# A hybrid decoder layer on one core: merge projection in three column passes with kept weights, first FFN-out group of five f-tiles, four f-tiles in the last stage

## The chip, the cores and the metric

The kernel runs on 1 core of one Trainium2 chip (trn2). The metric is the device time of one execution in microseconds (us), lower is better; for the kernel before it is the median of three runs. The engines are TensorE (PE; PEld is its weight load), VectorE (DVE), ScalarE (ACT), GpSimd (POOL) and SyncE (SP, which issues the transfers here).

## The reference

One inference step of a one-layer decoder trunk: 1024 prompt columns and 8 samples, width 1024, FFN width 2816. All in float32. The mixers (a Conformer convolution and a gated delta rule) are not touched by the change; what follows them is:

```
merged = jax.nn.sigmoid(m_a) * y_a + jax.nn.sigmoid(m_b) * y_b
x = x + gt1 * (merged @ w_merge_out)
h2 = rms_norm(x, norm2_g) * (1 + sc2) + sh2
gate, up = jnp.split(h2 @ w_ffn_in, 2, axis=-1)
x = x + gt2 * ((jax.nn.silu(gate) * up) @ w_ffn_out)
...
y = rms_norm(x, final_norm_g)
```

## The kernel before

Activations lie transposed: channels on 128 partitions, T = 1032 columns (8 samples, then the prompt). Width 1024 is 8 tiles, the FFN has 22 f-tiles. A float32 product is done as three matmuls on rounded operands, high x high, high x low, low x high (`passes`); so each weight and each activation needs a `split`: ScalarE writes the high half (L188), VectorE subtracts for the low half (L189). Columns are worked in three passes of 344 (`cols(n)`). A `product` of eight k-tiles is 24 matmuls of 344 columns.

Weights come through the class `Weights`: there is one buffer `raw` for what SP loads, `prepare` splits it and only then is the next load asked for; the halves go into a ring of two (`whi`, `wlo`) or, for a kept weight ("hl"), into slots `whk`, `wlk`. `get` hands out the next one. SP, VectorE, ScalarE and GpSimd run what a scheduler has put in order; PE's order is that of the code; in the last stage the orders of VectorE, ScalarE and GpSimd are written by hand too. `along` holds generators of side work (norms, output); `after()` and `unit()` step them between products, and a `yield` says how many steps to wait.

The stages that matter, in the order of time:

- Merge projection (`merge`): for each output tile m a product with `w_merge_out`, `residual` into x2 (L1284, with L1287 and L1288 for the samples), a square and its sum for the norm (`Norm.square`, L1300 and L1304), and a write of x2 to a DRAM tile `xD`. Columns 0 and 1 are done for all m first, then column 2. Six weights have to be found again for column 2: two were kept split (`WMO_HL`), two are still in the ring, four were kept unsplit (`WMO_RAW`) and are split a second time ("again").
- norm2: `sums` (16 matmuls, L1315 and L1316), `rstd`, `bcast` (8 matmuls, L1326), then `modulate2` writes h2 = ms. Columns 0 and 1 together, then column 2.
- FFN in (`seven`, L1494): each f-tile of `silu(gate) * up` is written to a DRAM tile `aD`, since it doesn't stay on the chip.
- FFN out: f-tiles in groups `FGROUPS`; the tiles of a group are read back (`act_load`: a DMA into `ub`, `act` or `ar`, then a split into `ah` and `al`), then for each output tile and column pass one product over the group and a residual. While a group runs, the tiles of the next are read back. x2 is read back from `xD` (`x2_load`, in the order `XO`).
- Last stage: the last `FL` f-tiles (weights `wfl`), in three column blocks of 400, 400 and 232 (L1656), each with residual, square and sum; the final norm and the output multiply (`finish`, L1642) of a block run beside the next block; the last block is multiplied at the end from `yl` (L1680).

Of the kernel before, what the change touches and what calls it, by code (L numbers as in the profile page):

```python
# [18 lines left out]
P = 128  # L19
NP = 1024  # L20
NS = 8
T = NP + NS
# [10 lines left out]
FGROUPS = (7, 6, 6)  # L33
# [3 lines left out]
WMO_RAW, WMO_HL = (0, 1, 2, 3), (4, 5)  # L37
AHEAD = 3
XO = (0, 4, 1, 5, 2, 6, 3, 7)
WFL_AT = (1, 3, 5)  # L40
# [24 lines left out]
def trunk_step(ctx, tc, I, O):  # L65
# [136 lines left out]
    order += [(I["wmo"][m], 1024, "raw" if m in WMO_RAW else "hl" if m in WMO_HL else "") for m in range(KD)]  # L202
    order += [(None, 1024, "again") for m in WMO_RAW]
# [3 lines left out]
    for i, nf in enumerate(FGROUPS):  # L207
        for m in range(KD):
            order2.append((I["wfo"][m][:, f0 * P:(f0 + nf) * P], nf * P))
            if i == len(FGROUPS) - 1 and m in WFL_AT:  # L210
                order2.append((I["wfl"][WFL_AT.index(m)], 1024, "hl"))
        f0 += nf

    class Weights:


        def __init__(self, order):
            self.order, self.loaded, self.ready, self.kept, self.at = order, [], [], [], 0

        def load(self):  # L220
            if self.at < len(self.order) and not self.loaded:
                src, n, kind = (self.order[self.at] + ("",))[:3]
                self.at += 1
                if kind == "again":
                    raw = self.kept.pop(0)
                else:
                    raw = slot_d("rawk") if kind == "raw" else wp.tile(
                        [P, 1024], F32, tag="aw" if kind == "aw" else "raw", name="raw", bufs=1)
                    SP.dma_start(raw[:, :n], src)
                self.loaded.append((raw, n, kind))  # L230

        def prepare(self, eng=V):
            if self.loaded and not self.ready:
                raw, n, kind = self.loaded.pop()
                if kind == "hl":
                    hi, lo = slot_d("whk", F32R), slot_d("wlk", F32R)
                else:
                    hi = wp.tile([P, 1024], F32R, tag="hi", name="whi")
                    lo = wp.tile([P, 1024], F32R, tag="lo", name="wlo")
                split(hi[:, :n], lo[:, :n], raw[:, :n], eng)  # L240
                if kind == "raw":
                    self.kept.append(raw)
                self.ready.append((hi, lo))
                self.load()
# [28 lines left out]
    def after():  # L273
        W.prepare()
# [1070 lines left out]
    def modulate2(cs):  # L1345

        c0, c1 = cs[0].start, cs[-1].stop
        c = slice(max(c0, NS), c1)
        for k in range(KD):
            yield 0  # L1350
            sh = mods[:, SH2, k, :]
            modulate(x2[k], norm2.rb, a2[:, k, :], sh, ms[k][0], ms[k][1], x2[k], c0, c1, V)
            A.activation(x2[k][:, c], x2[k][:, c], AF.Identity, bias=sh[:, 0:1])
# [9 lines left out]
    kept = {}  # L1363
    for m in range(KD):
        w = W.get()
        if m not in WMO_RAW:
            kept[m] = w
        for n in range(2):
            merge(m, w, n)
            after()  # L1370
    add(norm2.work((cols(0), cols(1)), modulate2), 0)
    late = [6, 7, 0, 1, 2, 3, 4, 5]
    norm2.first, norm2.last = late[0], late[-1]
    for m in late:
        w = kept.pop(m) if m in kept else W.get()
        after()
        merge(m, w, 2)
# [169 lines left out]
    def act_load(f, sl, raw=None):  # L1547
        raw = slot_l("ar") if raw is None else raw
        hi, lo = sl("ah", F32R), sl("al", F32R)
        SP.dma_start(raw, aD[f])  # L1550
        split(hi, lo, raw, V)
        acts.append((hi, lo))

# [6 lines left out]
    for f in range(NPL, NF + 1):  # L1560
# [5 lines left out]
        if f > NPL:  # L1566
# [14 lines left out]
            if f == NF:  # L1581

                act_load(6, slot_d, act[NF - 2])
                x2_load(XO[1:6])
            seven(f - 1, "S4", B22, c12)
            SP.dma_start(aD[f - 1], a_)
            if f == NF - 1:
                for i in range(4):
                    act_load(i, slot_h, (v, a_)[i % 2])
            if f == NF:  # L1590
                x2_load(XO[6:])
        if f < NF:
# [14 lines left out]
            if f == NF - 1:  # L1607
                for i in range(4, 6):
                    act_load(i, slot_d, (ub[NF % 2], act[NF - 2])[i % 2])
# [11 lines left out]
    for g, nf in enumerate(FGROUPS):  # L1621
        for m in range(KD):
            w = W.get()
            for n in range(3):
# [5 lines left out]
            if m < ahead[g]:  # L1630
                sl = slot_h if (m < 4 if g + 1 < len(FGROUPS) else m < 2) else slot_d
                act_load(f1 + m, sl)
# [5 lines left out]
    def finish(cs):  # L1638
        c = cs[0]
        for k in range(KD):  # L1640
            yield 1 if c.start == 0 or k < 2 else 0.5
# [6 lines left out]
    norm3 = Norm(range(KD), V, slot_h)  # L1648
    yl = [slot_h(f"yl{i}")[:, :4 * YL].rearrange("p (k t) -> p k t", k=4) for i in range(2)]
    for a, b in ((0, YC), (YC, 2 * YC), (2 * YC, T)):  # L1650
# [12 lines left out]
        if b < T:  # L1663
            unit()
            add(norm3.work((c,), finish, 2, 2), 1)
# [9 lines left out]
    left(3)  # L1675
# [3 lines left out]
    for i in range(2):  # L1679
        V.tensor_tensor(yl[i], yl[i], ps[:, None, :YL].broadcast_to((P, 4, YL)), ALU.mult)  # L1680
        SP.dma_start(O["y"][:, 4 * i:4 * i + 4, c], yl[i])
# [93 lines left out]
```

## Time and profile before

| what | value |
|---|---|
| median of three runs | 1593.66 us (1591.69 to 1596.32) |
| the profiled execution's own time | 1594.41 us |
| its span, first to last instruction | 1592.7 us |
| mean granted clock of TensorE | 0.981 of full speed |
| merge projection to the FFN, about | 745 to 855 us |
| FFN-out groups | 1298.6 to 1538.0 us |
| last stage | 1538.0 to 1592.7 us |

Views of one profiled execution give start times from the span's beginning. A granted clock of 1.00 is 2.4 GHz, one of 0.50 is 1.2 GHz. An engine's idle time is given in square brackets before an instruction, with what ended it.

### The profile page before, as it was taken

Reading aid. Unit: us, or ns where it says so; the run is one execution under the profiler, and the core shown is the slowest. Engines: PE = TensorE matmul, PEld = TensorE weight load, DVE = VectorE, ACT = ScalarE, POOL = GpSimd, SP = SyncE. Lnnn points to the kernel's source line nnn. Section 1 sums busy time; section 2 is a strip of 40 time slices with the busy share of each in tenths; the row PEclk is TensorE's granted clock in tenths of the full one; section 3 lists DMA queues with packets and bytes.
Section 4 is the critical chain, followed back from the end, with each engine's and each line's share of the span. In section 5 each row is a group of like instructions: output and inputs, shape, how many; then the busy total and the mean of one; then the engine's idle time right before and its main releaser. Section 6 shows DMA issues by size and latency. Waiting matters only on the chain.

```text
span 1592.7 us, 27503 instructions
## 1 busy us (share of the span) xinstructions
PE 1525.4 (96%) x11383; PEld 1460.2 (92%) x11383; DVE 988.2 (62%) x1958; ACT 571.8 (36%) x1025; POOL 37.6 (2%) x67
## 2 busy tenths in 40 slices
PE   6999999999999999999979999999999978999996
PEld 3888999998888889999979999999999967999996
DVE  3667776999993642227466766666666754344446
ACT  5785653234334512114254433333333322021113
POOL 1210000000030000000000000000000000000000
PEclk8999999999999999999999999999999988999998
DMA  9134333233433444115202122222222164141202
GB/s 370 41 105 105 117 101 91 80 88 107 128 111 114 160 140 143 40 53 182 73 35 71 67 81 80 81 80 80 81 81 80 54 247 144 45 130 54 81 19 107
DMA packets 83374, 161.18 MB, mean 101 GB/s; under 512 B 20113, under 2 KB 41265, under 8 KB 83249
## 3 DMA queue, kind: packets, MB, share of 16 engines
q1 hardware_dynamic: 83248, 159.43, 30.8%
q8 instruction: 89, 1.46, 0.4%
q14 instruction: 37, 0.30, 0.1%
HBM read 128.37 MB, written 31.04 MB: 100 GB/s over the span
## 4 chain that ended last, share of the span: by engine, by line
PE 80%; DVE 10%; DMA 4%; ACT 4%; issue 1%; POOL 1%; SPq 0%; DVEq 0%; ACTq 0%; POOLq 0%
PE mm L264 49%; PE mm L1494 25%; DVE ca L719 3%; DVE cv L546 1%; PE ada L974 1%; DMA act<-aD 1%; PE w L791 1%; DVE wlo L189 1%; DMA x<-xD 1%; DVE x L1284 1%; DMA adw<-in_wada_dram 1%; DMA x<-in_x_dram 1%; ACT sq L1300 1%; DVE sacc L1304 0%; DMA em<-gcd 0%
## 5 line engine op out<-in xcount | busy, mean ns | idle before, releaser
L264 PE MATMUL mm<-hh,whi 128*128 128x344 f32 x920 | 306.1, 333 | 0.0
L264 PE MATMUL mm<-hl,whi 128*128 128x344 f32 x920 | 296.1, 322 | 0.0
L264 PE MATMUL mm<-hh,wlo 128*128 128x344 f32 x920 | 295.5, 321 | 0.0
L264 PEld LDWEIGHTS mm<-hh,whi 128*128 128x128 f32 x920 | 174.1, 189 | 14.8 <-issue 13.5
L1494 PE MATMUL mm<-mh,fm 128*128 128x258 f32 x960 | 182.7, 283 | 0.0
L264 PEld LDWEIGHTS mm<-hl,whi 128*128 128x128 f32 x920 | 174.2, 189 | 0.0
L264 PEld LDWEIGHTS mm<-hh,wlo 128*128 128x128 f32 x920 | 174.1, 189 | 0.0
L188 ACT ACTIVATE whi<-raw 128x1024 fp32r<-128x1024 f32 (+2 forms) x78 | 78.3, 1004 | 244.2 <-PE mm L264 219.3
L264 PE MATMUL mm<-ah,whi 128*128 128x344 f32 x456 | 148.0, 325 | 15.1 <-ACT ah L188 12.5
L189 DVE TENSOR_TENSOR wlo<-raw,whi 128x1024 fp32r<-128x1024 f32 (+2 forms) x78 | 90.4, 1159 | 114.3 <-ACT whi L188 112.8
L1284 DVE SCALAR_TENSOR_TENSOR x<-mm,mods,x 128x344 f32<-128x344 f32 (+4 forms) x120 | 68.1, 569 | 139.9 <-PE mm L264 138.0
L1494 PEld LDWEIGHTS mm<-mh,fm 128*128 128x128 f32 x960 | 152.3, 189 | 0.0
L264 PE MATMUL mm<-al,whi 128*128 128x344 f32 x456 | 147.7, 324 | 2.4 <-DVE al L189 2.4
L719 DVE SCALAR_TENSOR_TENSOR ca<-u,par,ca 128x1017 f32<-128x1017 f32 (+26 forms) x120 | 148.4, 1261 | 1.9 <-ACT ca L716 1.3
L264 PE MATMUL mm<-ah,wlo 128*128 128x344 f32 x456 | 147.1, 323 | 0.0
L1494 PE MATMUL mm<-ml,fm 128*128 128x258 f32 x480 | 135.5, 282 | 0.0
L1494 PE MATMUL mm<-th,fm 128*128 128x258 f32 x640 | 121.7, 282 | 0.0
L1494 PE MATMUL mm<-t,fm 128*128 128x258 f32 x960 | 121.4, 282 | 0.0
L1494 PEld LDWEIGHTS mm<-t,fm 128*128 128x128 f32 x960 | 117.7, 189 | 0.0
L1499 DVE TENSOR_TENSOR ub<-mm,ub 128x258 f32<-128x258 f32 x160 | 67.5, 424 | 60.3 <-PE mm L1494 59.7
L264 PEld LDWEIGHTS mm<-ah,whi 128*128 128x128 f32 x456 | 86.5, 190 | 17.1 <-ACT ah L188 14.3
L1494 PEld LDWEIGHTS mm<-th,fm 128*128 128x128 f32 x640 | 101.9, 189 | 0.0
(421 smaller groups left out, 2888.4 us busy)
## 6 DMA issues: line engine op xcount, KB each, us to landing
raw<-in_win_dram SPq DMA_DIRECT2D x40, 512.0 KB, 3.9
aw<-in_wada_dram SPq DMA_DIRECT2D x32, 512.0 KB, 3.6
aD<-act SPq DMA_DIRECT2D x20, 516.0 KB, 3.7
x<-in_x_dram SPq DMA_DIRECT2D x16, 516.0 KB, 6.2
adw<-in_wada_dram SPq DMA_DIRECT2D x16, 512.0 KB, 9.5
ar<-aD SPq DMA_DIRECT2D x15, 516.0 KB, 3.5
raw<-in_wfo_dram SPq DMA_DIRECT2D x16, 384.0 KB, 3.1
aw<-in_wfi_dram SPq DMA_DIRECT2D x20, 256.0 KB, 3.0
```

What stands on the lines that cost most here:

```text
L188: A.activation(dst_hi, src, AF.Copy)
L189: eng.tensor_tensor(dst_lo, src, dst_hi.bitcast(F32), ALU.subtract)
L264: PE.matmul(ps[:, :NCH], l, r[:, c], start=k == first and i == 0, stop=k == last and i == 2)
L546: V.scalar_tensor_tensor(acc, *tap(t), acc, ALU.mult, ALU.add)
L719: V.scalar_tensor_tensor(acc[:, NS + d:T], u[:, 0:NP - d], w(d), acc[:, NS + d:T], ALU.mult, ALU.add)
L791: PE.matmul(b8(ps, r, h, n)[:, c * n:(c + 1) * n], lhsT(c), rhs(c), start=True, stop=True)
L974: PE.matmul(ps[32 * g:32 * g + 32, :256], cT[:, k, :], raw[:, g * 256:(g + 1) * 256], start=k == 0, stop=k == KD - 1)
L1284: V.scalar_tensor_tensor(xk[:, a:b], ps[:, o:b - c.start], gate[:, 0:1], xk[:, a:b], ALU.mult, ALU.add)
L1300: A.activation(d, x2[k][:, c], AF.Square)
L1494: PE.matmul(ps[:, :HC], l[:, w], r[:, c], start=k + i == 0, stop=k == 3 and i == 2)
L1499: V.tensor_tensor(dst, ps[:, :HC], src, ALU.add)
```

## The change

Three parts. The merge projection goes over the columns in three passes, n = 0, 1, 2; pass 0 takes each weight as it comes and all eight stay split until pass 2 (six in slots, the last two in the ring); no raw weight is kept. norm2 is then worked three times, once for each pass. The FFN-out groups become 5, 7, 6 f-tiles, which leaves four for the last stage; the first group goes over the output tiles in the order `XO` with one x2 tile read back for each, and tiles 0 and 3 of the activation are read back in three chunks. The last stage's norm buffers lie in other slots, its output is spaced by one step, and the last multiply and store are done in four pieces instead of two. The core of the diff:

```diff
-FGROUPS = (7, 6, 6)
+FGROUPS = (5, 7, 6)
 FL = NF - sum(FGROUPS)
...
-WMO_RAW, WMO_HL = (0, 1, 2, 3), (4, 5)
+WMO_HL = 6
...
-WFL_AT = (1, 3, 5)
+WFL_AT = (0, 2, 4, 6)
...
-    order += [(I["wmo"][m], 1024, "raw" if m in WMO_RAW else "hl" if m in WMO_HL else "") for m in range(KD)]
-    order += [(None, 1024, "again") for m in WMO_RAW]
+    order += [(I["wmo"][m], 1024, "hl" if m < WMO_HL else "") for m in range(KD)]
...
         for k in range(KD):
-            yield 0
+            yield 2 if c1 < T else 0
             sh = mods[:, SH2, k, :]
...
-    for m in range(KD):
-        w = W.get()
-        if m not in WMO_RAW:
-            kept[m] = w
-        for n in range(2):
-            merge(m, w, n)
-            after()
-    add(norm2.work((cols(0), cols(1)), modulate2), 0)
-    late = [6, 7, 0, 1, 2, 3, 4, 5]
-    norm2.first, norm2.last = late[0], late[-1]
-    for m in late:
-        w = kept.pop(m) if m in kept else W.get()
-        after()
-        merge(m, w, 2)
+    wm = []
+    for n in range(3):
+        ks = list(range(KD)) if n < 2 else list(range(WMO_HL, KD)) + list(range(WMO_HL))
+        norm2.first, norm2.last = ks[0], ks[-1]
+        for m in ks:
+            if n == 0:
+                wm.append(W.get())
+            merge(m, wm[m], n)
+            if n == 2 or n == 0 and m < KD - 1:
+                after()
+        if n < 2:
+            add(norm2.work((cols(n),), modulate2), 0)
...
+    def act_chunks(f):
+        raw = [chunk("ac") for _ in range(3)]
+        for n in range(3):
+            SP.dma_start(raw[n], aD[f, :, cols(n)])
+        return raw
...
             if f == NF:
-
-                act_load(6, slot_d, act[NF - 2])
-                x2_load(XO[1:6])
+                x2_load(XO[1:2])
             seven(f - 1, "S4", B22, c12)
             SP.dma_start(aD[f - 1], a_)
             if f == NF - 1:
-                for i in range(4):
-                    act_load(i, slot_h, (v, a_)[i % 2])
-            if f == NF:
-                x2_load(XO[6:])
+
+                act_load(0, slot_h, ac)
+                ac = act_chunks(3)
+                for i in (1, 2):
+                    act_load(i, slot_h, (a_, v)[i % 2])
+                act_load(3, slot_h, ac)
+        if f == NF - 2:
+            ac = act_chunks(0)
...
-                for i in range(4, 6):
-                    act_load(i, slot_d, (ub[NF % 2], act[NF - 2])[i % 2])
+                act_load(4, slot_d, ub[NF % 2])
...
-        for m in range(KD):
+        for j, m in enumerate(range(KD) if g else XO):
             w = W.get()
+            if g == 0 and j + 2 < KD:
+                x2_load(XO[j + 2:j + 3])
...
-            yield 1 if c.start == 0 or k < 2 else 0.5
+            yield 1
...
-    norm3 = Norm(range(KD), V, slot_h)
-    yl = [slot_h(f"yl{i}")[:, :4 * YL].rearrange("p (k t) -> p k t", k=4) for i in range(2)]
+    norm3 = Norm(range(KD), V, slot_l)
+    yl = [slot_d(f"yl{i}")[:, :4 * YL].rearrange("p (k t) -> p k t", k=4) for i in range(2)]
...
-            add(norm3.work((c,), finish, 2, 2), 1)
+            add(norm3.work((c,), finish, 1, 3), 1)
...
-    left(3)
+    left(2)
...
-    for i in range(2):
-        V.tensor_tensor(yl[i], yl[i], ps[:, None, :YL].broadcast_to((P, 4, YL)), ALU.mult)
-        SP.dma_start(O["y"][:, 4 * i:4 * i + 4, c], yl[i])
+    for i in range(4):
+        y_ = yl[i // 2][:, i % 2 * 2:i % 2 * 2 + 2, :]
+        V.tensor_tensor(y_, y_, ps[:, None, :YL].broadcast_to((P, 2, YL)), ALU.mult)
+        SP.dma_start(O["y"][:, 2 * i:2 * i + 2, c], y_)
```

**SP where the merge begins.** `raw` and `rawk` from `in_wmo` are the merge weights, the x2 tiles (`x20` to `x27`) come from `in_x`, and `xD` is what the merge writes out. The kernel before, in the order of issue (weights 0 and 1 were loaded long ahead; here are 2 to 7):

```order
L229 DMA rawk_7301<-in_wmo_dram 128x1024
L229 DMA rawk_7368<-in_wmo_dram 128x1024
L229 DMA raw_7437<-in_wmo_dram 128x1024
L1275 DMA x20_7234<-in_x_dram 128x1032
L229 DMA raw_7506<-in_wmo_dram 128x1024
L1275 DMA x21_7236<-in_x_dram 128x1032
L229 DMA raw_7575<-in_wmo_dram 128x1024
L1275 DMA x22_7238<-in_x_dram 128x1032
```

The changed kernel, weights 2 to 5:

```order
L224 DMA raw_7301<-in_wmo_dram 128x1024
L1268 DMA x22_7238<-in_x_dram 128x1032
L1268 DMA x23_7240<-in_x_dram 128x1032
L1268 DMA x27_7241<-in_x_dram 128x1032
L1268 DMA x24_7235<-in_x_dram 128x1032
L1268 DMA x25_7237<-in_x_dram 128x1032
L224 DMA raw_7340<-in_wmo_dram 128x1024
L1268 DMA x26_7239<-in_x_dram 128x1032
L1352 DMA xD_7232<-x20_7234 128x344
L1352 DMA xD_7232<-x21_7236 128x344
L224 DMA raw_7379<-in_wmo_dram 128x1024
L1352 DMA xD_7232<-x22_7238 128x344
```

Before, weights 2 to 6 all stand ahead of `x22` and of the five x loads behind it; now weight 3 (`raw_7340`) stands behind five x loads, and weight 4 (`raw_7379`) behind the writes of tiles 0 and 1.

**VectorE in the merge's first pass.** L1284 (L1277 in the changed file) is the residual, L1304 (L1297) the sum of squares, `wlo` and `wlk` the low half of a weight. Before:

```order
L1284 SCALAR_TENSOR_TENSOR x21_7236<-mm_7370,mods_149,x21_7236 128x344
L189 TENSOR_TENSOR wlo_7434<-rawk_7368,whi_7433 128x1024
L1304 TENSOR_TENSOR sacc_7264<-sacc_7264,sq_7396 128x344
L1284 SCALAR_TENSOR_TENSOR x22_7238<-mm_7400,mods_149,x22_7238 128x336
L1287 TENSOR_TENSOR rs8_7426<-mm_7400,mods_149 128x8
L1288 TENSOR_TENSOR x22_7238<-x22_7238,rs8_7426 128x8
L1304 TENSOR_TENSOR sacc_7264<-sacc_7264,sq_7429 128x344
L1284 SCALAR_TENSOR_TENSOR x22_7238<-mm_7439,mods_149,x22_7238 128x344
L189 TENSOR_TENSOR wlo_7641<-raw_7575,whi_7640 128x1024
```

After, from tile 3 to tile 5:

```order
L1277 SCALAR_TENSOR_TENSOR x23_7240<-mm_7381,mods_149,x23_7240 128x336
L1280 TENSOR_TENSOR rs8_7407<-mm_7381,mods_149 128x8
L1281 TENSOR_TENSOR x23_7240<-x23_7240,rs8_7407 128x8
L1297 TENSOR_TENSOR sacc_7264<-sacc_7264,sq_7410 128x344
L1277 SCALAR_TENSOR_TENSOR x24_7235<-mm_7420,mods_149,x24_7235 128x336
L1280 TENSOR_TENSOR rs8_7446<-mm_7420,mods_149 128x8
L189 TENSOR_TENSOR wlk_7454<-raw_7418,whk_7453 128x1024
L1281 TENSOR_TENSOR x24_7235<-x24_7235,rs8_7446 128x8
L1297 TENSOR_TENSOR sacc_7264<-sacc_7264,sq_7449 128x344
L1277 SCALAR_TENSOR_TENSOR x25_7237<-mm_7459,mods_149,x25_7237 128x336
L1280 TENSOR_TENSOR rs8_7485<-mm_7459,mods_149 128x8
L189 TENSOR_TENSOR wlo_7493<-raw_7457,whi_7492 128x1024
```

Between two low halves stood two residuals (two column passes of one tile); now there is one, and the low half of weight 5 (`wlk_7454`) stands behind the residual of tile 4, that of weight 6 (`wlo_7493`) behind tile 5's.

**SP at the readback.** `ub`, `act`, `ar` and `ac` take activations from `aD`, `raw` a weight of the first group, `x20` to `x27` the x2 tiles from `xD`. Before:

```order
L1586 DMA aD_7233<-act_12887 128x1032
L1550 DMA ub0_8183<-aD_7233 128x1032
L1550 DMA act_12887<-aD_7233 128x1032
L1550 DMA ub0_8183<-aD_7233 128x1032
L229 DMA raw_13362<-in_wfo_dram 128x896
L1557 DMA x20_13272<-xD_7232 128x1032
L1557 DMA x24_13311<-xD_7232 128x1032
L1550 DMA act_12887<-aD_7233 128x1032
L1557 DMA x21_13313<-xD_7232 128x1032
L1557 DMA x25_13315<-xD_7232 128x1032
L1557 DMA x22_13317<-xD_7232 128x1032
L1557 DMA x26_13319<-xD_7232 128x1032
```

After:

```order
L1552 DMA ac_13147<-aD_7233 128x344
L1552 DMA ac_13148<-aD_7233 128x344
L1552 DMA ac_13149<-aD_7233 128x344
L1585 DMA aD_7233<-act_12909 128x1032
L1542 DMA ub0_8199<-aD_7233 128x1032
L1542 DMA act_12909<-aD_7233 128x1032
L1542 DMA ub0_8199<-aD_7233 128x1032
L224 DMA raw_13374<-in_wfo_dram 128x640
L1558 DMA x20_13301<-xD_7232 128x1032
L1558 DMA x24_13335<-xD_7232 128x1032
L1558 DMA x21_13376<-xD_7232 128x1032
L1542 DMA ar_13438<-aD_7233 128x1032
```

Before, the fourth tile stood behind two x loads, and three more tiles of the first group follow the rows shown, behind these x loads; after, all five tiles of the first group are asked for before the first x load, and `ar_13438` already belongs to the second group.

## Rows read from the trace of the kernel before

**Rows 1.** The page: span, and busy time, share and instructions of each engine.

```profile
span 1592.7 us, 27503 instructions
...
PE 1525.4 (96%) x11383; PEld 1460.2 (92%) x11383; DVE 988.2 (62%) x1958; ACT 571.8 (36%) x1025; POOL 37.6 (2%) x67
```

**Rows 2.** What PE waited for, 800 us to the end: total, times, longest (us).

```profile
PE mm L264 <- ACT ah L188: 12.5, 4, 4.3
PE mm L264 <- DVE wlo L189: 8.0, 1, 8.0
...
PE mm L264 <- DVE act L1499: 2.6, 1, 2.6
```

**Rows 3.** Windows around the hole in the merge; columns as headed.

```profile
core 0: us, PE busy (x) PEld busy (x) DVE busy (x) ACT busy (x) POOL busy (x), PEclk, DMA share, GB/s
...
820.20:828.20 8.00, 0.01 (x1) 0.01 (x1) 8.00 (x17) 7.54 (x10) 0.00 (x0) 0.78 0.06 22
828.20:831.70 3.50, 3.50 (x13) 3.50 (x14) 3.50 (x8) 2.73 (x5) 0.00 (x0) 0.52 0.14 50
```

**Rows 4.** Windows of the FFN-out groups and the last stage, columns the same.

```profile
1298.64:1301.20 2.56, 0.00 (x1) 0.00 (x0) 1.54 (x3) 0.95 (x1) 0.00 (x0) 1.00 0.97 385
1301.20:1326.70 25.50, 10.48 (x31) 7.29 (x32) 9.60 (x13) 7.11 (x8) 0.00 (x0) 0.53 0.74 273
1326.70:1538.00 211.30, 211.30 (x1339) 211.30 (x1338) 85.42 (x155) 35.78 (x38) 0.00 (x0) 1.00 0.26 79
1538.00:1592.70 54.70, 41.84 (x290) 39.75 (x288) 36.06 (x80) 17.72 (x38) 0.00 (x0) 0.91 0.22 78
```

**Rows 5.** Timeline of one kept weight on SP, ACT, DVE: start, duration, instruction.

```profile
726.63 0.33 SPq L229 DMA_DIRECT2D raw<-in_wmo_dram  x1
...
730.23 1.06 ACT L188 ACTIVATE whk<-raw 128x1024 fp32r<-128x1024 f32 x1 [1.70 <-DMA raw<-in_wmo_dram]
...
731.33 1.23 DVE L189 TENSOR_TENSOR wlk<-raw,whk 128x1024 fp32r<-128x1024 f32 x1
```

**Rows 6.** A window of the merge's first products, columns as in rows 3.

```profile
754.00:756.00 2.00, 2.00 (x15) 2.00 (x14) 1.22 (x1) 0.33 (x1) 0.00 (x0) 1.00 0.42 158
```

**Rows 7.** Timeline of DVE at the merge's first residual.

```profile
749.25 0.57 DVE L1284 SCALAR_TENSOR_TENSOR x<-mm,mods,x 128x336 f32<-128x336 f32 x1 [0.73 <-PE mm L264]
```

**Rows 8.** Timeline of PE, two holes of nearly the same length earlier on.

```profile
95.39 0.38 PE L496 MATMUL gc<-gates,gg 128*32 128x128 f32 x2 [1.90 <-DVE bg L492]
...
373.33 1.29 PE L902 MATMUL ds<-vh,kd 128*128 128x128 f32 x8 [1.94 <-DVE kd L865]
```

**Rows 9.** Windows behind these two holes, columns as in rows 3.

```profile
95.40:100.00 4.60, 4.60 (x28) 4.15 (x29) 3.71 (x12) 3.73 (x8) 0.00 (x0) 1.00 0.35 116
374.20:377.60 3.40, 3.40 (x17) 3.40 (x16) 3.40 (x6) 2.52 (x2) 0.00 (x0) 0.50 0.08 12
```

**Rows 10.** Timeline of PE at norm2's broadcast for the last column pass.

```profile
855.66 1.02 PE L1326 MATMUL rb<-rr,sel 128*128 128x86 f32 x8
856.47 0.41 PE L264 MATMUL mm<-mh,whi 128*128 128x344 f32 x1
```

**Rows 11.** Timeline of ACT and DVE at the readback.

```profile
1298.68 0.95 ACT L188 ACTIVATE whi<-raw 128x896 fp32r<-128x896 f32 x1 [2.83 <-PE mm L1494]
...
1299.66 1.09 DVE L189 TENSOR_TENSOR wlo<-raw,whi 128x896 fp32r<-128x896 f32 x1 [2.21 <-ACT whi L188]
...
1315.33 1.06 ACT L188 ACTIVATE ah<-act 128x1032 fp32r<-128x1032 f32 x1 [5.44 <-DMA act<-aD]
```

**Rows 12.** Transfers, 1255 to 1345 us: count, KB each, median us to landing.

```profile
x<-xD SPq DMA_DIRECT2D x8, 516.0 KB, 10.0
```

**Rows 13.** Timeline of PE at the start of the last stage.

```profile
1538.01 0.35 PE L1656 MATMUL mm<-ah,whk 128*128 128x400 f32 x1
...
1538.92 0.34 PE L1656 MATMUL mm<-ah,wlk 128*128 128x400 f32 x1
```

**Rows 14.** The chain that ended last, in the last stage: start, us, engine, line.

```profile
1569.86 0.37 DVE x L1284
...
1587.36 1.03 DVE yl L1680
```

More of the change, by code (lines that the diff above doesn't have):

```diff
@@ L207, in trunk_step @@
     for i, nf in enumerate(FGROUPS):
-        for m in range(KD):
+        for m in (range(KD) if i else XO):
             order2.append((I["wfo"][m][:, f0 * P:(f0 + nf) * P], nf * P))
@@ L217, in __init__ @@
         def __init__(self, order):
-            self.order, self.loaded, self.ready, self.kept, self.at = order, [], [], [], 0
+            self.order, self.loaded, self.ready, self.at = order, [], [], 0
         def load(self):
@@ L223, in load @@
                 self.at += 1
[L224 to L229, printed above, removed]
+                raw = wp.tile([P, 1024], F32, tag="aw" if kind == "aw" else "raw", name="raw", bufs=1)
+                SP.dma_start(raw[:, :n], src)
                 self.loaded.append((raw, n, kind))
@@ L240, in prepare @@
                 split(hi[:, :n], lo[:, :n], raw[:, :n], eng)
-                if kind == "raw":
-                    self.kept.append(raw)
                 self.ready.append((hi, lo))
@@ L1362, in trunk_step @@
     norm2 = Norm(range(KD), V, slot_l)
-    kept = {}
-    for m in range(KD):
-        w = W.get()
-        if m not in WMO_RAW:
-            kept[m] = w
-        for n in range(2):
-            merge(m, w, n)
-            after()
-    add(norm2.work((cols(0), cols(1)), modulate2), 0)
-    late = [6, 7, 0, 1, 2, 3, 4, 5]
-    norm2.first, norm2.last = late[0], late[-1]
-    for m in late:
-        w = kept.pop(m) if m in kept else W.get()
-        after()
-        merge(m, w, 2)
+    wm = []
[10 more added lines that the diff above has]
+            add(norm2.work((cols(n),), modulate2), 0)
     h2 = ms
@@ L1548, in act_load @@
         raw = slot_l("ar") if raw is None else raw
+        if not isinstance(raw, list):
+            raw = [raw]
+            SP.dma_start(raw[0], aD[f])
         hi, lo = sl("ah", F32R), sl("al", F32R)
-        SP.dma_start(raw, aD[f])
-        split(hi, lo, raw, V)
+        w = T // len(raw)
+        for i, r in enumerate(raw):
+            split(hi[:, i * w:(i + 1) * w], lo[:, i * w:(i + 1) * w], r, V)
         acts.append((hi, lo))
+    def act_chunks(f):
[3 more added lines that the diff above has]
+        return raw
     def x2_load(ks):
@@ L1621, in trunk_step @@
     for g, nf in enumerate(FGROUPS):
-        for m in range(KD):
+        for j, m in enumerate(range(KD) if g else XO):
             w = W.get()
+            if g == 0 and j + 2 < KD:
+                x2_load(XO[j + 2:j + 3])
             for n in range(3):
@@ L1629, in trunk_step @@
                     wfl.append(W.get())
-            if m < ahead[g]:
-                sl = slot_h if (m < 4 if g + 1 < len(FGROUPS) else m < 2) else slot_d
-                act_load(f1 + m, sl)
+            if j < ahead[g]:
+                act_load(f1 + j, slot_h if j < 4 else slot_d)
         f0 += nf
```

## Prediction

> **What bounds the kernel now.** The page first: TensorE is busy 96% of the span and the next engine, VectorE, 62% [rows 1]. So the kernel is a queue of matmuls, and time can come only from matmuls not run, from matmuls run at the low clock, or from holes in PE. I therefore read next, from 800 us on, the list of what PE waited for [rows 2]: 12.5 us in four holes for `ah` (ScalarE's high half of an activation tile read back from memory), 8.0 us in one hole for `wlo` (VectorE's low half of a weight), 2.6 us for an activation. Everything else there is small. Third, I cut the two stretches where those holes lie into windows with their granted clock. Around the 8.0 hole [rows 3] PE does one matmul in 8.00 us while VectorE is busy all of it, and the 3.50 us after run 13 matmuls at a clock of 0.52. In the readback [rows 4] PE is empty for 2.56 us, then for 25.50 us it is busy only 10.48 and runs 31 matmuls at 0.53; after it come 211.30 us with 1339 matmuls at clock 1.00, which gives 211.30 / 1339 = 0.1578 us for each 344-column matmul. The last stage takes 54.70 us.
>
> **Merge projection.** A product is 24 matmuls (8 k-tiles, three passes): 24 x 0.1578 = 3.79 us. Before, each new weight serves two column passes, 7.6 us of PE. After, in pass 0, one: 3.79.
> Removed: splitting the four raw weights again before the third pass. That is where VectorE was full while PE stood: 8.0 us, and the 13 slow matmuls after it cost 3.50 - 13 x 0.1578 = 1.4 more. Gain 9.4. In its place the third pass finds all eight weights split; passes 1 and 2 need no weight.
> Added: what a kept weight costs, from [rows 5]. There is one `raw` buffer, so the chain is serial: load issued at 726.63, ScalarE starts on it at 730.23, VectorE at 731.33 and ends at 732.56, when the next load can go. 732.56 - 726.63 = 5.93 us per weight against 3.79 of PE. The order on VectorE says the same another way: the low half of weights 5, 6 and 7 stands behind the residual of the tile before, so product (3.79), residual (0.57 [rows 7]) and low half (1.23) follow one another, 5.6 and some semaphore time. Both say that PE waits 5.93 - 3.79 = 2.1, I take 2.2, at each of weights 4 to 7: 8.8 us. Nothing covers it: there is no second product. Weight 3 is loaded behind five x loads (order of SP). Before, those transfers fill the DMA engines until about 754.8 (busy 0.42 of the window 754 to 756 [rows 6]), nine us after the merge starts; weight 3 would be wanted after three products, 11.4 us, and needs its two halves, 1.06 + 1.23, after landing: I take 0.9 of a hole there, between 0 and 3. Together 9.7.
> Clock: a hole of about 2 us is on the edge. The one of 1.94 us at 373.33 [rows 8] is followed by a window at clock 0.50; the one of 1.90 at 95.39 by one at 1.00 [rows 9]. At half clock 3.40 us of work are 1.7 lost. I take that for two of the four holes: 3.4, between 0 and 6.8 if they stay single events.
> One norm more: the broadcast moves the next matmul from 855.66 to 856.47 [rows 10], 0.8; the sixteen sums taken alike, 1.6 together. ScalarE's and VectorE's norm work lies beside 30 us of products without weights in each of passes 1 and 2, so it costs nothing; if that cover failed, the FFN's first products would wait for `h2`.
> The `xD` writes on SP wait for residuals, and weight loads 4 to 7 stand behind them; each such residual is of an earlier tile than the one PE works on, so it adds nothing beyond the chain.
> Sum of this part: -9.4 + 9.7 + 3.4 + 1.6 = +5.3.
>
> **Readback and groups.** Before, 2.56 + 25.50 + 211.30 = 239.4 us [rows 4] for 3 x 8 x 3 x 19 = 1368 matmuls, which by themselves are 215.9. After, 18 f-tiles: 1296 matmuls, 204.5. The first product needs five tiles instead of seven. Before, the later tiles of the seven landed late, behind x loads (ScalarE waited 5.44 us for one, at 1315.33 [rows 11]). Now the five that are needed stand ahead of all x loads on SP, two of them in chunks, and the sixth and seventh are wanted only after 8 x 3 x 5 x 3 = 360 matmuls, 57 us later. The x loads, one of which took 10.0 us to land in that crowd [rows 12], now come one per output tile behind the activations. So I expect the four holes for `ah` gone. What stays is the first hole: ScalarE and VectorE split the first weight (0.95 and 1.09 [rows 11]) while the activation that PE needs stands behind it on VectorE. With 640 columns instead of 896 these shrink by 0.27 and 0.31: 2.56 - 0.58 = 2.0. Half of the slow stretch of 1.7 behind it: 0.9. 204.5 + 2.0 + 0.9 = 207.4, so -32.0.
>
> **Last stage.** Four f-tiles instead of three in columns 400/400/232. Matmuls of 400 columns follow each other at (1538.92 - 1538.01) / 5 = 0.182 us [rows 13]. Before, PE needs 9 x 0.182 = 1.64 a tile, but block 2's first residual begins at 1569.86 [rows 14], 31.86 after the start: 1.99 for each of 16 tiles, VectorE's pace (residual, square's sum, output multiply). After, 12 x 0.182 = 2.18 is above that pace, so PE sets it: 16 x 2.18 = 34.9, norm matmuls 1.6, the first product of block 2 at 232/400 of the length 1.3, and about 1 of VectorE work still standing: 38.8. From there to the end was 1592.70 - 1569.86 = 22.84 on VectorE's chain, unchanged. The last multiply and store (1.03 at 1587.36) are cut into halves, so the last transfer starts with half the bytes: of the 4.3 us from that multiply's end to the end of the span I take off 1.0, between 0 and 2.1. 38.8 + 21.8 = 60.6 against 54.7: +5.9.
>
> **Sum.** 1592.7 + 5.3 - 32.0 + 5.9 = 1571.9 span. The profiled execution's own time is 1594.41, 1.7 above its span, and the median 1593.66 is 0.75 below that: 1571.9 + 1.7 - 0.75 = 1572.9, I say 1573. Own range 1567 to 1580 (holes in pass 0 between 1.5 and 3 us each, none or all of them followed by the low clock).
>
> **Rivals.**
> B, pass 0 without holes: if the chain's stations overlap more than the trace of one busy weight shows, PE never waits, and the 8.8 and 3.4 fall away: 1573 - 12.2, about 1561. For it: VectorE has far less to do than in the old stretch. Against: one `raw` buffer, and the chain is made of pure durations.
> C, the clock stays low through weights 3 to 7: at half clock a product takes 24 x 3.50 / 13 = 6.5 us [rows 3], and residual, low half and semaphores (2.2) still follow it: 8.7 a weight instead of 5.9, five times 2.8 = 14.0, less the 3.4 counted: about 1584. For it: 1.94 us sufficed once; against: 1.90 did not, and the holes here stand between bursts of 3.8 us of dense matmuls.
> The Trainium skill's page "TensorE: Matmul & The Clock Gate", section "HAM oscillation — how this bites in real kernels", speaks for C: in a loop that waits for a transfer at every step, the clock falls in each wait and each step begins at the low level. The trace agrees as to single holes (1.94 us, clock 0.50 after), not as to all of them; no run here shows a row of such holes yet.
> D, the change doesn't do what it says: two of the five tiles still land late, one period of 5.44 + 1.06 = 6.5 us each [rows 11]: +13, 1586. For it: three tiles still go through the last 15 us of the stage before; against: the three first read back then had landed before the hole.
> E, slower: the crowd moves to pass 0. If each load of weights 3 to 7, now among x loads and `xD` writes, took 10.0 us as the x load did [rows 12] instead of 3.6, the period is 12.3 instead of 5.9: five times 6.4 = +32, 1605. It decides from a landing of 3.6 + (1594 - 1573) / 5, about 7.8 us. Against: the x loads end at 754.8 and nothing heavy follows.
>
> **Chances.** Forecast 0.60, B 0.14, C 0.14, D 0.07, E 0.05. The time is the forecast's. From 1560 to 1586 stand nearly all of the forecast, half of B, nearly all of C and half of D: about 0.8. A measurement here tells changes of over 0.3% (4.8 us) from none: faster is below 1588.9, all of the forecast and B and most of C and D, 0.91; within 0.3%: what is left of C and D and a mild E, 0.04; slower, E, 0.05.
>
> **What would show it.** In pass 0 four PE holes of about 2 us, released by VectorE's low half, none of 8 us; the windows behind them tell the forecast (some at 1.00) from C (all near 0.5). In the first group one hole of about 2 us for `act`, and none for `ah`; about 207 us from the first group's start to the last stage, about 61 in the last stage with PE dense in two blocks. It would be wrong if weight loads in pass 0 land in more than 5 us, if `ah` returns to the waits, or if the FFN's start waits for `h2`.

## The result and the profile after

The changed kernel runs in 1567.18 us (median of four, 1566.62 to 1569.59) against 1593.26 for the kernel before (median of four): a ratio of 0.9837, 95% interval 0.9819 to 0.9855, faster by 26 us. The forecast was 1573 with a range of 1560 to 1586; of the narrower range that the prediction calls its own, 1567 to 1580, the time is at the lower edge. The profiled execution took 1566.97 with a span of 1565.2.

The list of what PE waited for from the merge to the end, changed kernel:

```profile
core 0 of [0], span 1565.2 us
engine line waited for: us in total, times, longest us
PE mm L257 <- DVE wlk L189: 2.1, 2, 1.4
PE mm L257 <- DVE wlo L189: 2.0, 2, 1.4
PE rs L1308 <- DVE sacc L1297: 1.5, 1, 1.5
PE mm L257 <- ACT whi L188: 1.4, 1, 1.4
PE rb L1319 <- DVE rr L306: 1.1, 1, 1.1
PE mm L257 <- ACT whk L188: 1.1, 1, 1.1
PE rs L1309 <- ACT sq L1293: 1.1, 1, 1.1
PE mm L257 <- DVE act L1489: 0.8, 1, 0.8
```

Beside [rows 2]: the 12.5 us for `ah` and the 8.0 us for one `wlo` are gone; new are 6.6 us in front of weight halves (the four lines with `wlk`, `wlo`, `whi`, `whk`: low and high halves), and the hole for `act` is 0.8 instead of 2.6.

Windows by stage, changed kernel: merge projection to the first form of the FFN, the forms, the FFN-out groups, the last stage. Columns: from:to, length, then the busy time and instructions of PE, PEld, DVE, ACT, POOL, then PE's granted clock, DMA share and GB/s.

```profile
742.82:895.59 152.77, 146.06 (x938) 142.66 (x938) 91.69 (x199) 65.17 (x121) 0.00 (x0) 0.98 0.28 94
895.59:1298.75 403.16, 403.16 (x3362) 402.95 (x3360) 275.70 (x576) 135.02 (x268) 0.00 (x0) 1.00 0.25 83
1298.75:1504.10 205.35, 204.60 (x1296) 204.63 (x1297) 93.86 (x170) 41.39 (x45) 0.00 (x0) 1.00 0.36 115
1504.10:1565.20 61.10, 51.59 (x362) 50.30 (x360) 37.26 (x82) 17.79 (x38) 0.00 (x0) 0.93 0.20 70
```

The same first stretch of the kernel before:

```profile
745.26:895.38 150.12, 142.12 (x939) 141.16 (x938) 93.86 (x184) 64.85 (x109) 0.00 (x0) 0.98 0.23 79
```

The columns to compare are the lengths. Merge 152.77 against 150.12: +2.65, on as many matmuls. The forms 403.16 against 1298.64 - 895.38 = 403.26: -0.1. Groups 205.35 against 239.4 [rows 4]: -34.0, now dense (1296 matmuls in 204.60 busy, clock 1.00). Last stage 61.10 against 54.70 [rows 4]: +6.4. And the merge begins at 742.82 instead of 745.26: -2.4 in a part that the change doesn't touch. Together -27.5, which is the difference of the spans, 1592.7 - 1565.2.

The new holes, one by one. The timeline of PE at weights 4 and 5 of the first column pass:

```profile
759.58 0.42 PE L257 MATMUL mm<-mh,whk 128*128 128x344 f32 x1 [1.08 <-ACT whk L188]
...
760.84 0.52 PE L257 MATMUL mm<-mh,wlk 128*128 128x344 f32 x1 [0.68 <-DVE wlk L189]
...
767.97 0.43 PE L257 MATMUL mm<-mh,wlk 128*128 128x344 f32 x1 [1.41 <-DVE wlk L189]
```

And the chain that feeds them, on SP, ACT and DVE:

```profile
753.50 1.23 DVE L189 TENSOR_TENSOR wlk<-raw,whk 128x1024 fp32r<-128x1024 f32 x1 [2.08 <-ACT whk L188]
...
754.75 0.33 SPq L224 DMA_DIRECT2D raw<-in_wmo_dram  x1
...
758.48 1.06 ACT L188 ACTIVATE whk<-raw 128x1024 fp32r<-128x1024 f32 x1 [2.05 <-DMA raw<-in_wmo_dram]
...
759.56 1.23 DVE L189 TENSOR_TENSOR wlk<-raw,whk 128x1024 fp32r<-128x1024 f32 x1 [2.58 <-ACT whk L188]
...
766.15 0.57 DVE L1277 SCALAR_TENSOR_TENSOR x<-mm,mods,x 128x336 f32<-128x336 f32 x1 [3.54 <-PE mm L257]
```

The load goes out at 754.75, two hundredths after the low half of weight 3 has read the buffer (753.50 + 1.23); 3.73 later ScalarE starts, 1.08 later VectorE. This is the serial chain of [rows 5]. The loads that follow it on SP, of weights 5, 6, 7 and of the FFN's first weight:

```profile
760.82 0.33 SPq L224 DMA_DIRECT2D raw<-in_wmo_dram  x1
767.95 0.33 SPq L224 DMA_DIRECT2D raw<-in_wmo_dram  x1
774.31 0.33 SPq L224 DMA_DIRECT2D raw<-in_wmo_dram  x1
781.43 0.33 SPq L224 DMA_DIRECT2D raw<-in_wfi_dram  x1
```

From load to load weights 4 to 7 take 6.07, 7.13, 6.36 and 7.12 us. PE begins a weight as soon as its high half is there, runs two matmuls and stands again for the low half: so weight 4 costs two holes, 1.08 and 0.68. At weight 5 the other lock holds: the low half stands behind the residual at 766.15, which waits for PE's own product; that makes this period 7.13 instead of about 6. The holes at weights 4 to 7 are 1.8, 1.4, 2.1 and 1.4 us, 6.6 in all.

Weight 3, whose load went out at 744.06 among the x loads, took 8.35 us to ScalarE's start, and PE met it with nothing to spare:

```profile
744.06 0.38 SPq L224 DMA_DIRECT2D raw<-in_wmo_dram  x1
...
752.41 1.06 ACT L188 ACTIVATE whk<-raw 128x1024 fp32r<-128x1024 f32 x1 [4.20 <-DMA raw<-in_wmo_dram]
...
754.78 0.42 PE L257 MATMUL mm<-mh,wlk 128*128 128x344 f32 x1
```

The matmul ahead of this one began at 754.32, so the step is 0.46 instead of 0.16. And since the buffer came free only then, weight 4 was asked for late too.

### The profile page after: what moved, and what is told of

Same layout as the page of the kernel before. It is cut to its first block, busy times and chain, and to the rows that moved or that the text cites. A ratio compares the mean times of both kernels' runs of the same rounds, so it can differ in the third digit from the quotient of the medians.

```text
span 1565.2 us, 27552 instructions
## 1 busy us (share of the span) xinstructions
PE 1518.3 (97%) x11383; PEld 1455.2 (93%) x11383; DVE 986.5 (63%) x1977; ACT 572.3 (37%) x1042; POOL 37.7 (2%) x67
## 4 chain that ended last, share of the span: by engine, by line
PE 80%; DVE 10%; DMA 4%; ACT 3%; issue 1%; POOL 1%; SPq 0%; DVEq 0%; ACTq 0%; POOLq 0%
PE mm L257 47%; PE mm L1484 25%; DVE ca L712 3%; PE mm L1659 2%; DMA raw<-in_wmo_dram 1%; DVE cv L539 1%; PE ada L967 1%; DVE wlo L189 1%; PE w L784 1%; DMA adw<-in_wada_dram 1%; DMA x<-in_x_dram 1%; DMA em<-gcd 0%; DVE wlk L189 0%; ACT whi L188 0%; DVE hl L334 0%
## 5 line engine op out<-in xcount | busy, mean ns | idle before, releaser
L188 ACT ACTIVATE whi<-raw 128x1024 fp32r<-128x1024 f32 (+3 forms) x78 | 77.4, 992 | 227.3 <-PE mm L257 186.8
L189 DVE TENSOR_TENSOR wlo<-raw,whi 128x1024 fp32r<-128x1024 f32 (+3 forms) x78 | 89.3, 1144 | 112.8 <-ACT whi L188 112.0
L1277 DVE SCALAR_TENSOR_TENSOR x<-mm,mods,x 128x344 f32<-128x344 f32 (+4 forms) x120 | 68.3, 569 | 124.8 <-PE mm L257 114.2
L257 PE MATMUL mm<-ah,whi 128*128 128x344 f32 x432 | 138.4, 320 | 0.8 <-DVE act L1489 0.8
L257 PE MATMUL mm<-al,whi 128*128 128x344 f32 x432 | 138.3, 320 | 0.0
L257 PE MATMUL mm<-ah,wlo 128*128 128x344 f32 x432 | 138.1, 320 | 0.0
L1484 PE MATMUL mm<-tl,fm 128*128 128x258 f32 x320 | 90.7, 284 | 0.0
```

What stands on the lines that cost most here:

```text
L188: A.activation(dst_hi, src, AF.Copy)
L189: eng.tensor_tensor(dst_lo, src, dst_hi.bitcast(F32), ALU.subtract)
L257: PE.matmul(ps[:, :NCH], l, r[:, c], start=k == first and i == 0, stop=k == last and i == 2)
L1277: V.scalar_tensor_tensor(xk[:, a:b], ps[:, o:b - c.start], gate[:, 0:1], xk[:, a:b], ALU.mult, ALU.add)
L1484: PE.matmul(ps[:, :HC], l[:, w], r[:, c], start=k + i == 0, stop=k == 3 and i == 2)
```

## The experiments

Each starts from the changed kernel unless it says otherwise. Ratios are against the kernel before, run on the same chip beside it.

**1. The old merge, the rest changed.** Edit, the merge alone put back:

```diff
-WMO_HL = 6
+WMO_RAW, WMO_HL = (0, 1, 2, 3), (4, 5)
...
-    for n in range(3):
...
+    for m in range(KD):
+        w = W.get()
...
+        for n in range(2):
+            merge(m, w, n)
+            after()
```

> The changed kernel with only its merge projection put back to that of the kernel before (two column passes, then a third with four weights split again); groups and last stage stay changed. Theory: the new merge is a net loss of 2.6 us, as the two traces show from the merge's first product to the FFN's first form (152.8 us after, 150.1 before), so this runs at about 1564.5 us, with one hole of about 8 us ahead of the third pass and none in the first. Rival 1: the prediction's own size, a loss of 5.3, gives 1562. Rival 2: the new merge gains, and the early prefetches of weights cost something elsewhere: above 1567.

Measured: 1563.42 us, ratio 0.9817 (0.9796 to 0.9839). Its windows have the stretch from the merge to the forms:

```profile
742.76:892.78 150.02, 142.03 (x938) 141.01 (x937) 93.86 (x184) 64.86 (x109) 0.00 (x0) 0.98 0.25 82
```

150.02 against 152.77, as the theory said; its one wait of PE there is the 8.0 for `wlo`. The intervals of the two whole-time ratios overlap, so the loss by the new merge stands on the stretches, where it repeats: the new merge takes 152.77 in the changed kernel and 152.64, 153.36, 153.42, 152.69 and 153.20 in experiments 4, 5, 6, 7 and 9, which leave it as it is; the old one takes 150.12 and 150.25 (experiment 10) in the kernel before and 150.02 here. The loss is 2.4 to 3.4 us. The second rival is out; the first, 1562, isn't told apart by the time but by the stretch.

**2. Two column passes together, all eight weights kept.** The merge's loops:

```diff
...
+    for m in range(KD):
+        wm.append(W.get())
+        for n in range(2):
+            merge(m, wm[m], n)
+            if m < KD - 1:
+                after()
+    add(norm2.work((cols(0), cols(1)), modulate2), 0)
+    late = [6, 7, 0, 1, 2, 3, 4, 5]
+    norm2.first, norm2.last = late[0], late[-1]
+    for m in late:
+        merge(m, wm[m], 2)
+        after()
...
-            yield 2 if c1 < T else 0
+            yield 0
```

> The changed kernel, but pass 0 and pass 1 of the merge run together again (each new weight serves two column passes one after the other), while all eight weights stay split for the third pass. Theory: the holes of the first pass come from one product (3.8 us) per weight against a chain of 6 to 7 us; two products (7.6) cover it, and nothing is split again ahead of the third pass, so neither the four holes nor the 8 us hole is there: from the merge's first product to the FFN's first form 140.7 us instead of 152.8, time about 1555. Rival: norm2 and the modulation of two column passes then fall on VectorE all at once in the third pass, residuals stand behind them, and PE waits there 3 to 8 us with a low clock after: 1559 to 1565.

Measured: 1556.07 us, ratio 0.977 (0.9751 to 0.9788). Windows, then what PE waited for from the merge to the forms:

```profile
743.15:885.54 142.39, 140.66 (x938) 139.71 (x937) 89.69 (x183) 61.47 (x105) 0.00 (x0) 1.00 0.31 101
```

```profile
PE mm L257 <- DVE x L1277: 1.7, 1, 1.7
```

142.39, between theory (140.7) and rival: all weight holes are gone, and what the rival named is there but small: PE waits once, 1.7 us, for a residual that stands behind the modulation on VectorE. The clock of the stretch is 1.00.

**3. Weights 4 to 7 not loaded.** It leaves out four loads; weight 3 is split in their place.

```diff
...
+                if self.wmo0 + 4 <= self.at - 1 < self.wmo0 + KD:
+                    raw = self.last
+                else:
+                    raw = wp.tile([P, 1024], F32, tag="aw" if kind == "aw" else "raw", name="raw", bufs=1)
+                    SP.dma_start(raw[:, :n], src)
+                self.last = raw
...
```

> The changed kernel with the loads of merge weights 4 to 7 left out: weight 3, which is already there, is split in their place, so every split and product is still done, on other numbers. Theory: the serial chain through the one buffer is set by the load (about 4.0 of 6.4 us); without it all four holes go and with them the low clock: 12 us less, about 1555. Rival: VectorE's order sets them (the low half stands behind the residual of the tile before): holes of about 1.4 us stay at each weight, no low clock after them, about 1561.

One run: 1556.39 us. Windows and waits from the merge to the forms:

```profile
743.19:884.75 141.56, 141.22 (x938) 139.76 (x937) 91.37 (x198) 64.75 (x121) 0.00 (x0) 1.00 0.25 87
```

```profile
PE mm L263 <- DVE wlk L189: 0.3, 1, 0.3
```

The splits, the products and the three norms are all still there, and 152.77 - 141.56 = 11.2 us go with the loads, holes and slow stretches both (clock 1.00). It isn't a pure test of the load chain against VectorE's order: without the loads the scheduler also moved the low halves of weights 4 to 7 ahead on VectorE, the last of them ends at 760.4. So both locks went at once, and the share of each isn't shown by this run; that the order can hold PE too is seen at weight 5 above.

**4. x2 loads asked for early again.**

```diff
             if f == NF:
-                x2_load(XO[1:2])
+                x2_load(XO[1:6])
             seven(f - 1, "S4", B22, c12)
             SP.dma_start(aD[f - 1], a_)
+            if f == NF:
+                x2_load(XO[6:])
...
-            if g == 0 and j + 2 < KD:
-                x2_load(XO[j + 2:j + 3])
```

> The changed kernel with the x2 loads of the first group asked for where the kernel before asked for them (five ahead of the last f-tile's fourth form, two behind it) instead of one per output tile; the group still has five tiles. Theory: what removed the readback's holes is that the first group asks for only five tiles, all ahead of the x loads in time: no hole for ah, 1567. Rival: the moved x loads removed them: a hole of 3 to 5 us for ah returns, with the low clock behind it, 1572 to 1580.

Measured: 1567.51 us, ratio 0.984 (0.9822 to 0.9857), no wait for `ah`. The x loads on SP in this run:

```profile
1291.84 1.33 SPq L1558 DMA_DIRECT2D x<-xD  x3
...
1293.79 2.31 SPq L1558 DMA_DIRECT2D x<-xD  x4
...
1298.55 0.32 SPq L1558 DMA_DIRECT2D x<-xD  x1
```

The cause is plainer than the theory: SP's order is the same as in the changed kernel, x load for x load (there three at 1293.15, four at 1295.15, one at 1299.96). The scheduler puts these loads there wherever of the two places the code asks for them, so this part of the change did nothing, and this edit can't say what their place is worth. It also means that the x loads never came one per output tile: all eight go out within 7 us, in the kernel before within 10 (1292.96 to 1302.46).

**5. No chunks.** Tiles 0 to 3 are read back whole:

```diff
-                act_load(0, slot_h, ac)
-                ac = act_chunks(3)
-                for i in (1, 2):
-                    act_load(i, slot_h, (a_, v)[i % 2])
-                act_load(3, slot_h, ac)
-        if f == NF - 2:
-            ac = act_chunks(0)
+                for i in range(4):
+                    act_load(i, slot_h, (v, a_)[i % 2])
```

> The changed kernel, group of five, but tiles 0 to 3 of the first group are read back whole through the two buffers that the kernel before used, instead of tiles 0 and 3 in three chunks ahead of time; the fourth tile then stands behind two x2 loads on SP and the fifth behind six, as in the kernel before. Theory: a group of five alone isn't enough, the chunks put its five tiles ahead of the crowd: holes for ah of about 2.5 and 5 us at the fourth and fifth tile return, with 2 to 4 us of low clock: about 1578. Rival: five tiles are few enough: no hole over 1 us, 1567.

Measured: 1578.95 us, ratio 0.9899 (0.9877 to 0.992). What PE waited for in the groups, and two windows (all groups; the slow stretch):

```profile
PE mm L257 <- ACT ah L188: 5.8, 2, 4.2
PE mm L257 <- DVE al L189: 1.5, 2, 0.8
```

```profile
1302.60:1517.47 214.87, 207.62 (x1298) 206.30 (x1297) 95.11 (x169) 43.30 (x47) 0.00 (x0) 0.98 0.35 115
1306.50:1316.70 10.20, 4.81 (x14) 4.00 (x15) 2.89 (x6) 1.97 (x2) 0.00 (x0) 0.50 0.94 378
```

The groups take 214.87 against 205.35: the chunks, with the earlier place on SP that they give the five tiles, are worth 9.5 us. The holes for `ah` are 5.8 in sum, in two, nearly as the theory had it, and they lie in 10.2 us at a clock of 0.50; PE's busy time is 207.62 against 204.60. The rival is out.

**6. Seven tiles first.** As 5, with groups of 7, 5, 6 and tiles 5 and 6 loaded as in the kernel before.

```diff
-FGROUPS = (5, 7, 6)
+FGROUPS = (7, 5, 6)
...
-                act_load(4, slot_d, ub[NF % 2])
+                for i in range(4, 6):
+                    act_load(i, slot_d, (ub[NF % 2], act[NF - 2])[i % 2])
```

> As the run without chunks, and with groups of 7, 5 and 6, so that the first group waits for seven tiles as before, while the last stage and the merge stay changed. Theory: the sixth and seventh tile land last, some 12 us behind the fifth as in the kernel before, all holes for ah are back (about 12 us in them, clock near 0.5 through them): about 20 us above the changed kernel, 1587, of which 9 beyond the run without chunks. Rival: the moved x2 loads (written one per output tile, here too) let them land in time: under 1575.

Measured: 1593.62 us, ratio 0.9991 (0.9981 to 1.0): the gain is gone.

```profile
PE mm L257 <- ACT ah L188: 15.4, 4, 5.5
PE mm L257 <- DVE al L189: 2.7, 4, 0.8
```

```profile
1297.80:1528.14 230.34, 210.98 (x1297) 208.22 (x1297) 95.95 (x171) 43.24 (x47) 0.00 (x0) 0.95 0.33 107
```

The groups take 230.34, 25.0 more than in the changed kernel (20 were expected), 15.5 more than in 5. The four holes of [rows 2] are back, 15.4 us against 12.5. The mechanism held, the size was short.

**7. Three f-tiles in the last stage.** `FGROUPS = (5, 7, 7)`, `WFL_AT = (1, 3, 5)`.

> The changed kernel with groups of 5, 7 and 7, so that three f-tiles stay for the last stage. Theory: there a fourth tile costs less than in a group, because the last stage with three runs at VectorE's pace: 72 matmuls more in the groups, +11.4, and the last stage back from 61.1 to 54.7, -6.4: 1572. Rival: TensorE bounds both places, a matmul costs the same in either: 1567 within 1.5.

Measured: 1572.73 us, ratio 0.9861 (0.9845 to 0.9877). Windows of the groups and the last stage:

```profile
1301.95:1518.04 216.09, 215.94 (x1370) 215.96 (x1369) 92.49 (x168) 41.17 (x44) 0.00 (x0) 1.00 0.34 109
1518.04:1572.45 54.41, 41.44 (x290) 39.45 (x288) 36.28 (x82) 17.71 (x38) 0.00 (x0) 0.91 0.22 79
```

216.09 - 205.35 = +10.7 and 54.41 - 61.10 = -6.7: the fourth tile in the last stage brings 4.0 us by the stretches, where the theory had 5.0; the rival, no difference, is out.

**8. As 2, with the modulation spaced.** `yield 3 if c1 < T else 0` in place of `yield 0`.

> The run with two column passes together and all weights kept, with norm2's modulation of the first two passes spaced by three steps over the third pass instead of all at once. Theory: the one hole left in the merge there (1.73 us, PE waits for a residual that stands behind the modulation on VectorE) goes: 1554.3. Rival: the modulation then ends too late and the FFN's first product waits for h2, 2 us or more: 1556 to 1560.

Measured: 1556.62 us, ratio 0.976 (0.9746 to 0.9775).

```profile
745.57:886.44 140.87, 140.67 (x938) 139.71 (x938) 89.46 (x183) 61.27 (x105) 0.00 (x0) 1.00 0.31 102
```

140.87 us: the hole of 1.7 is gone (PE waits 0.2 there) and the FFN doesn't wait, as the theory had it, though not the time that it gave: 1556.62 instead of 1554.3 lies in the rival's range, without the wait that the rival named. The medians of 2 and 8 don't differ by what the runs can tell; the stretch does, by 1.5. This execution reached the merge 2.4 us later than that of experiment 2 (745.57, 743.15), in the part that neither changes.

**9. The last multiply in two pieces.** The two lines of the kernel before in place of the four-piece loop.

> The changed kernel with the last multiply and store in two pieces of 928 columns instead of four of 464. Theory: only the last transfer changes, from 2.65 to about 3.25 us, so from the first yl multiply to the end of the span 0.6 us more than the changed kernel's 5.8 (1559.41 to 1565.2). Rival, the prediction's value: 1.0 more; second rival, none, since four issues on SP cost what the smaller transfer gives.

One run: 1568.75 us. From the first `yl` multiply (1560.61) to the end of the span (1567.0) it takes 6.4 us, in the changed kernel 5.8 (1559.41 to 1565.2): the four pieces are worth 0.6, by one execution of each.

**10. The kernel before, once more.**

> The kernel before, unchanged, profiled once more, to see how much the clock in the 740 us ahead of the merge, which the change doesn't touch, moves one execution. Theory: the 2.4 us by which the changed kernel reached the merge earlier are low-clock stretches that come and go between 240 and 260 us: the merge starts anywhere from 741 to 747 us here, with 0 to 3 such stretches of 3.4 us; the 8.0 us hole, the holes of the readback and their low clock are the same as in the first profile within 1 us. Rival: the change itself brings the earlier start, so this one starts at 745.3 within 0.5.

One run: 1591.03 us, span 1589.3. Its merge begins at 741.67, and between 230 and 262 us, which no edit touches, it differs from the first profile of the same kernel:

```profile
230.00:262.00 32.00, 32.00 (x462) 30.38 (x462) 14.98 (x21) 10.44 (x22) 0.00 (x0) 0.89 0.45 113
```

```profile
230.00:262.00 32.00, 32.00 (x497) 30.54 (x496) 15.98 (x22) 11.09 (x23) 0.00 (x0) 1.00 0.45 112
```

The first row is the first profile, the second this one: PE is busy all of both, at 0.89 and at 1.00 of the clock, with 462 and 497 matmuls (partly others, since the second row's execution is ahead by then). The rival falls: the early start isn't the change's. The merge to the forms is 150.25 us here (150.12), the 8.0 us hole is 8.0 again, and the holes for `ah` sum to 13.1 (12.5); only the hole for `act` isn't the same, 1.4 against 2.6, so that the theory's "within 1 us" misses there by 0.2.

## Why the prediction was right, step by step

The direction and the mechanisms held, and no rival came whole. Part of the nearness is luck, and is named below. The terms of its sum, with what they measured:

- Merge, forecast +5.3, measured +2.65, and +2.75 against experiment 1. Gain from not splitting again: 9.4 forecast; 150.02 in experiment 1 against 140.87 in experiment 8 makes 9.15. The cost of pass 0: 9.7 in holes and 3.4 of clock forecast, 13.1; with the loads left out 11.2 go, and against experiment 8 it is 11.9. The single period (forecast 5.9, seen 6.07 and 6.36 where nothing but the load holds the weight) and the two low stretches were right in the changed kernel's profile:

```profile
761.00:764.40 3.40, 3.40 (x13) 3.40 (x14) 1.02 (x4) 0.49 (x1) 0.00 (x0) 0.50 0.66 194
768.50:771.50 3.00, 3.00 (x21) 2.92 (x19) 0.52 (x1) 0.08 (x1) 0.00 (x0) 1.00 0.77 223
774.70:778.10 3.40, 3.40 (x14) 3.40 (x13) 0.52 (x1) 0.23 (x1) 0.00 (x0) 0.50 0.67 198
782.00:785.00 3.00, 3.00 (x21) 3.00 (x20) 0.52 (x1) 0.06 (x1) 0.00 (x0) 1.00 0.71 216
```

  These are the windows behind weights 4, 5, 6 and 7: 0.50, 1.00, 0.50, 1.00. That two of four would be low was the prediction's middle between none and all, and that it came out so is luck: the same merge shows two low stretches in experiments 4 and 6, but one in 5, 7 and 9. There the holes add up to more, 8.0 to 8.4 us. What PE waited for in the merge of experiment 5:

```profile
PE mm L257 <- ACT whk L188: 2.5, 3, 1.3
PE mm L257 <- ACT whi L188: 2.4, 2, 1.2
PE mm L257 <- DVE wlk L189: 2.0, 3, 0.7
PE mm L257 <- DVE wlo L189: 1.4, 2, 0.7
```

  That is 8.3 us in holes with one low stretch, against 6.6 with two, and yet the whole stretch takes nearly the same, 153.36 and 152.77. So the step that was mis-sized is that holes and low clock were added as if they were independent. A product at the low clock runs longer while the chain goes on, so the hole behind it is shorter (1.4 us at weights 5 and 7 of the changed kernel, against 1.7 to 2.0 at all of weights 4 to 7 in experiment 5). The hole of 0.9 at weight 3 came in three of the six profiles (0.95, 0.68 and 0.95 us in experiments 5, 7 and 9), in the changed kernel only as the step of 0.46 above.
- The extra norm, forecast +1.6, is a step that was wrong in its reading. The windows have 938 matmuls after and 939 before: a norm over two column passes issues its matmuls for each of them, and so three norms of one pass issue as many as one of two and one of one. The 0.8 of [rows 10] is the price of one pass, not of one norm: in the changed kernel the broadcasts move the next matmul by 0.81, 0.81 and 0.80, in experiment 8 by 1.70 and 0.81. The third norm costs about nothing.
- Groups, forecast -32.0, measured -34.0. 11.4 of this are 72 matmuls fewer, which the last stage takes over. The holes for `ah` went, as said; of the reasons given, the tiles that come in chunks (9.5, experiment 5) and five tiles instead of seven (15.5, experiment 6) carry it. The reason that x loads come one per output tile was wrong, they don't (experiment 4). The remaining hole was taken as 2.0 with 0.9 of clock; it is 0.75 with none behind. Its 2.6 in the profile of before was itself large: the second profile has 1.4.
- Last stage, forecast +5.9, measured +6.4. PE is dense in blocks 0 and 1, as said: the only waits of that stage in the list are those of the final norm (`rs`, `rb`), behind the last product. But two errors offset each other. Block 2's first residual on VectorE begins 38.1 us into the stage (38.8 forecast; 1542.18 - 1504.10), and from there to the end it takes 23.0 instead of 21.8. The cut of the last store gives 0.6 instead of 1.0, and VectorE's chain from that residual to the first `yl` multiply, taken as unchanged, is longer by 0.8 (1559.41 - 1542.18 = 17.2, before 1586.25 - 1569.78 = 16.5); no run shows why.
- 2.4 us of the miss, 1565.2 against a forecast span of 1571.9, are of no term: the execution that the sum was made against had low-clock stretches between 230 and 262 us that the changed kernel's doesn't have. They come and go: over the twelve profiles of this case the clock of that window is 1.00 in five, 0.95 in four (experiments 1, 3, 8 and 9), 0.89 in the first of the kernel before and 0.84 in two (experiments 5 and 7). The merge starts at 741.2 to 743.2 us in the five and at 745.3 to 746.2 in the three below 0.9, with the same products ahead of it.

Rival C came in part: the clock fell behind two of the four holes, not all, and a weight took 6.1 to 7.1 us, not 8.7. The Trainium skill's page "TensorE: Matmul & The Clock Gate", section "HAM oscillation — how this bites in real kernels", describes the fall in a loop with a wait at every step, the waits there longer than these. The trace agrees for weights 4 and 6 (0.50), not for 5 and 7 (1.00). Rival E came for one load: weights 4 to 7 took 3.7 to 4.1 us to ScalarE's start, weight 3 took 8.35, more than the 5 that the prediction gave as a sign of being wrong. In the changed kernel the hole at weight 3 itself was small, but the crowd did cost something. With a landing like weight 4's the buffer would have come free some 4.6 us earlier (8.35 - 3.73), and weight 4 would have been split at about 756, before PE asked for it at 758.3. By this estimate the 1.8 us at weight 4 are the crowd's; no run tests it.

What the experiments point to: the merge of experiments 2 and 8 with the changed groups and last stage is the fastest version run, 1556 us. The change's three-pass merge is its weak part. Keeping all eight weights split is what pays; giving each new weight only one product takes the gain back.

## What to carry to other kernels

When a pass is cut into more passes, compare the PE time that one new weight feeds with the serial time of its chain (load, split, split, buffer free): 3.8 against 6.1 to 7.1 us cost 11 to 12 us here, 7.6 left no hole. Look in the issue order before you price a move of loads in the code: here the scheduler undid it. A term priced per event (a norm) should be checked by counting instructions, and a hole and the low clock behind it shouldn't be added where a longer product eats the next hole.

## What the runs showed of the hardware

TensorE's granted clock fell with PE busy by the profile and no wait listed: between 230 and 262 us two profiles of one kernel show 0.89 and 1.00. In the first of them the clock is low in two stretches:

```profile
241.00:244.40 3.40, 3.40 (x12) 3.09 (x12) 0.83 (x2) 1.46 (x4) 0.00 (x0) 0.51 0.32 48
254.70:258.10 3.40, 3.40 (x20) 3.03 (x19) 2.82 (x4) 1.21 (x3) 0.00 (x0) 0.50 0.97 375
```

Ahead of each, PE had run 96 small matmuls of 32x32 (`z`, L791, 2.65 us from 238.28 and from 251.30); the second profile has the same blocks and no fall, so what decides it stays open. A single execution's start of a late stage is thus uncertain by some 2 to 3 us either way, which is as much as the merge's loss; stretches from stage to stage are the better measure. And the length of a hole alone didn't decide what follows: in the changed kernel 1.8 us (in two pieces) was followed by 0.50 and 1.4 us by 1.00, while [rows 8] has 1.90 with 1.00 behind and 1.94 with 0.50 [rows 9].
